# Next block's small parameters and weight diagonals made inside the expert loop, and the second layer's end norm in two VectorE steps

## The chip, the cores and the metric

The kernel runs on one core of one Trainium2 chip. The metric is the device time of one execution in microseconds (us); of several runs the median counts. TensorE does the matrix products, VectorE the elementwise work with two operands, ScalarE activations and casts, GpSimd a third share of elementwise work and the indirect gathers; SyncE's queue issues nearly all other DMA transfers. Each engine works through its own instructions in a fixed order.

## The reference

A stack of three blocks for 512 tokens of width 1024, all in float32. Two layers of a first kind (three mixers side by side, then a mixture of experts), and one of a second kind. What the change touches is the end of each first-kind layer:

```python
for l in range(2):
    ...
    x = _layernorm(DEEPNORM_ALPHA * x + mix, ln1_g[l], ln1_b[l])
    ffn = _hier_moe(x, ...)            # 16 experts, 2 per token, weighted sum
    x = _layernorm(DEEPNORM_ALPHA * x + ffn, ln2_g[l], ln2_b[l])
# second block:
h = rmsnorm(x, norm_mix_w_2)           # x is needed too, for the residual
proj = h @ w_in_2
```

## The kernel before

Tokens lie in four tiles (NT = 4) of 128 partitions, `R[:, i]` being one tile of 128x1024 values. Matrix products are made of three passes on values split in a high and a low part (lines 122 to 124); a weight unit is loaded as float32 into `raw`, cast by ScalarE to the high part (line 132) and subtracted by VectorE or GpSimd for the low part (line 137). A few weight units sit in rings, and a cast waits until TensorE has let go of the ring's oldest unit.

`layer(l)` does one first-kind layer. After the routing (`route`, lines 1146 and following) it emits the loop of 16 experts: for each expert the 96 token rows are gathered by GpSimd from `Xd` (line 1072), transposed by TensorE (line 1079), run through gate, up and down products, and stored to `Yd` by SyncE (line 2038). The loop is software-pipelined: step `s` issues the gather of expert `s`, the transposes of `s-1`, the gate and up products of `s-2` and the down products of `s-3`.

Behind the loop, in program text, stand the small things of the next block. `cols` (lines 150 to 161) loads some rows of 128 values into one buffer `colr` (line 155), transposes them on TensorE into the PSUM pool `tr`, which the experts' transposes use too (line 158), and copies them out on VectorE (line 160); `colr` has one buffer, so each `cols` waits until the one before it has been transposed. `gc2` holds the norm's columns. `params(l + 1)` (line 1926) is eight or so small loads and two more `cols`, `cw` and `gcol`. In the second layer there are also the diagonals `dg`: eight 128x128 tiles, the identity times one token weight, made by GpSimd (line 2066) from the routing weights `w`.

Instructions are not run in the order of the text: a scheduler places each on its engine's queue when its own model of time says that the operands are there, and takes what stands first in the text when several are ready. So an instruction can be placed far ahead of its place in the text, and text order is a priority.

Behind a conditional block for overflowing experts (line 2072) comes the end of the layer. GpSimd gathers each token's two expert rows from `Yd` (line 2085). In the second layer token tiles 0 and 1 are summed on VectorE (lines 2091 and 2092), tiles 2 and 3 on TensorE with the diagonals (line 2099) and added by VectorE (line 2100). Then `moments` (line 440) makes the negative mean `nm`, the sum of squares on ScalarE (line 450) and the inverse deviation `rs` on VectorE in eight small steps (lines 169 to 177). The normed value is made by VectorE's product `nm*rs` (2104), ScalarE's Identity pass (2105), VectorE's product with the gain (2110) and GpSimd's sum with the bias (2111). ScalarE squares that (line 1308), VectorE makes the inverse root mean square, GpSimd the diagonal `rd` from it (2114), and `to_T` (line 336) transposes the tile with `rd` on TensorE (347) and splits it on ScalarE and VectorE (356, 357). The first loads of the next weights are gated (line 225): they wait until the last token tile's buffer `Yg[3][0]`, in which line 1308 also leaves its squares, is free.

Of the kernel before, what the change touches and what calls it, by code (L numbers as in the profile page):

```python
# [11 lines left out]
AF = mybir.ActivationFunctionType  # L12
OP = mybir.AluOpType
AX = mybir.AxisListType

P = 128
S = 512
NT = S // P
D = 1024
KD = D // P  # L20
# [48 lines left out]
class Kernel:  # L69
# [1894 lines left out]
    def layer(self, l):  # L1964
        nc, tc, a, v = self.nc, self.tc, self.a, self.nc.vector
# [3 lines left out]
        with ExitStack() as c:  # L1969
            mo = self.pool(c, f"moe{l}")  # L1970
# [4 lines left out]
            if l:  # L1975

                gb = [self.t(mo, "Ye", [P, D], bufs=2) for _ in range(2)]
# [8 lines left out]
            gb = halves()  # L1986
            gb = [gb[:, z] for z in range(2)]
# [3 lines left out]
            rw, bias, gc = self.router_weights(l, mo)  # L1991
# [42 lines left out]
            wts, rows, PM, cnt = self.route(mo, LG)  # L2034
            n = nc.values_load(cnt[0:1, 0:1], min_val=0, max_val=S)

            ex = {}
            store = lambda e: lambda y: nc.sync.dma_start(self.Yd[e * CAP:e * CAP + CAP, :], y)
            for s in range(16 + 4):
                if s == 8 and l == 0:  # L2040
                    self.level_masks(self.t(mo, "GTh", [P, KD, P], bufs=2))
                if s == 0:
                    self.pat = [("act", "dve")]

                if s < 16:
                    idx = self.slot_ids(mo, PM[:, s, :], 0, "idx")
                    ex[s] = self.expert(mo, [self.part((l, z, s)) for z in "gud"], idx, store(s))
                    next(ex[s])
                for z in (1, 2, 3):
                    if s - z in ex:  # L2050
                        next(ex[s - z])
            if l == 1:
                gb = halves()
                gb = [gb[:, z] for z in range(2)]
                for t, nm in zip(gb, ("ln2_g", "ln2_b")):
                    self.bcast_load(t, a[nm][l], D)
            fp = lambda ap: ap.rearrange("(f p) -> f p", p=P)
            if l == 0:
                gc = self.cols(self.ppool, "gc2", [fp(a["ln2_g"][l]), fp(a["ln2_b"][l])], 2 * KD)
            else:  # L2060
                gc = self.cols(self.ppool, "gc2", [fp(a["norm_mix_w_2"][0])], KD, 2 * KD)

                dg = self.t(mo, "dg", [P, 2, NT, P])
                for j in range(2):
                    for i in range(NT):
                        nc.gpsimd.tensor_tensor(dg[:, j, i], self.ident, wts[j][:, i:i + 1].to_broadcast([P, P]), op=OP.mult)
            self.params(l + 1)
            self.set_phase("m", [self.raw0], [self.ring0], [("act", "dve")])
            x2.close()
            x2 = ExitStack()  # L2070
# [17 lines left out]
            for i in range(NT):  # L2088
                r = R[:, i]
                if l == 0 or i < 2:  # L2090
                    v.scalar_tensor_tensor(r, Yg[i][0], wts[0][:, i:i + 1], r, op0=OP.mult, op1=OP.add)
                    v.scalar_tensor_tensor(r, Yg[i][1], wts[1][:, i:i + 1], r, op0=OP.mult, op1=OP.add,
                                           accum_out=sums[:, i, 0:1])
                else:
                    for hf in range(2):
                        py = self.ps(("pg", "py")[hf], [P, 512])
                        hs = slice(hf * 512, (hf + 1) * 512)
                        for j in range(2):
                            nc.tensor.matmul(py, dg[:, j, i], Yg[i][j][:, hs], start=j == 0, stop=j == 1)
                        v.scalar_tensor_tensor(r[:, hs], py, 1.0, r[:, hs], op0=OP.mult, op1=OP.add,  # L2100
                                               accum_out=sums[:, i, hf:hf + 1])
                nm, rs = self.moments(mo, r, sums[:, i, 0:1 if l == 0 or i < 2 else 2], Yg[i][0], 0.5e-5, nc.gpsimd if i < 2 and l == 0 else v)
                xh = Yg[i][1]
                v.tensor_tensor(nm, nm, rs, op=OP.mult)
                nc.scalar.activation(xh, r, AF.Identity, scale=rs, bias=nm)
                if l == 0:
                    nc.sync.dma_start(self.X2d[tok(i), :], xh)
                    self.to_T(XT, xh, i, gc=gc[:, 0:KD], bc=gc[:, KD:2 * KD], pool=mo)
                    continue
                v.tensor_tensor(r, xh, gb[0], op=OP.mult)  # L2110
                nc.gpsimd.tensor_tensor(r, r, gb[1], op=OP.add)
                rs = self.rms(mo, None, r, None, jk=Yg[i][0])
                rd = self.t(mo, "ehh", [P, 2, P], bufs=2)[:, 0]
                nc.gpsimd.tensor_tensor(rd, self.ident, rs.to_broadcast([P, P]), op=OP.mult)
                nc.sync.dma_start(self.X2d[tok(i), :], r)
                self.dump("x2_1", r, i)
                self.to_T(XT, r, i, gc=gc, pool=mo, rs=rd)
# [34 lines left out]
```

## Time and profile before

| what | before |
|---|---|
| median of 3 runs | 1753.94 us (1753.11 to 1755.02) |
| the profiled execution's own time | 1757.97 us |
| its span, first to last instruction | 1756.2 us |
| TensorE busy | 1598.3 us (91%) |
| VectorE busy | 1157.4 us (66%) |
| ScalarE busy | 808.5 us (46%) |
| GpSimd busy | 646.7 us (37%) |
| mean granted TensorE clock | 0.952 of full speed |

Times in the rows are microseconds from the start of the span. PE is TensorE, PEld its weight load, DVE VectorE, ACT ScalarE, POOL GpSimd, SPq SyncE's queue. L2104 is line 2104 of the kernel. "x4" behind a row counts instructions. What stands in brackets behind a row of a timeline is how long the engine was idle before it, and what ended that.

### The profile page before, as it was taken

The page shows a single profiled execution, that of the slowest core. Times are in us where ns is not written, and L with a number is a line of the kernel's source. Part 1 is how long each engine was busy: PE and PEld are TensorE (multiplying, and loading weights), DVE is VectorE, ACT ScalarE, POOL GpSimd, SP SyncE. Part 2 cuts the span into 40 slices and gives each one's busy share as a digit, 9 for nine tenths or more (in the row PEclk, how much of TensorE's full clock was granted, in tenths as well). Part 3 has the DMA queues.
Part 4 walks back from the last instruction along what each step waited for, and adds up shares of the span by engine and source line. Part 5 has one row for each costly group of instructions (what it writes and reads, how often), then busy time and mean ns, then how long its engine had stood idle before and what let it go on. Part 6 is the DMA issues. An engine that isn't in the chain of part 4 may idle for free. (4 is left out here: it accounts for less than half of the span.)

```text
span 1756.2 us, 28416 instructions
## 1 busy us (share of the span) xinstructions
PE 1598.3 (91%) x11003; PEld 1393.3 (79%) x11003; DVE 1157.4 (66%) x2327; ACT 808.5 (46%) x1396; POOL 646.7 (37%) x515
## 2 busy tenths in 40 slices
PE   7899999799976999998889995999798899999997
PEld 6789889788965789888879973887578788888886
DVE  3866963789967947865689977778774543333334
ACT  3344562267855344551358874465442432222221
POOL 1455331315005445334325204117533534444440
PEclk9999999889997999998989997999899999999999
DMA  5213324499956211124399964432112423333301
GB/s 156 85 58 111 98 76 120 171 340 365 374 185 211 76 57 35 61 84 135 124 336 356 378 238 154 126 96 73 38 51 85 148 92 96 96 96 96 96 25 48
DMA packets 126839, 247.95 MB, mean 141 GB/s; under 512 B 27180, under 2 KB 90470, under 8 KB 114406
## 3 DMA queue, kind: packets, MB, share of 16 engines
q1 hardware_dynamic: 120806, 225.05, 37.4%
q0 software_dynamic: 5888, 20.97, 3.8%
q8 instruction: 90, 1.47, 0.3%
q14 instruction: 55, 0.45, 0.1%
HBM read 218.21 MB, written 27.79 MB: 140 GB/s over the span
## 5 line engine op out<-in xcount | busy, mean ns | idle before, releaser
L137 POOL TENSOR_TENSOR wl<-raw,wh 128x1024 fp32r<-128x1024 f32 (+4 forms) x157 | 360.4, 2309 | 520.1 <-ACT wh L132 510.2
L132 ACT CAST wh<-raw 128x1024 fp32r<-128x1024 f32 (+3 forms) x361 | 362.6, 1023 | 295.5 <-PE dn L124 98.3
L137 DVE TENSOR_TENSOR wl<-raw,wh 128x1024 fp32r<-128x1024 f32 (+3 forms) x204 | 241.7, 1209 | 32.2 <-ACT wh L132 31.5
L122 PE MATMUL mm<-wh,actTh 128*128 128x256 f32 (+2 forms) x640 | 191.6, 300 | 12.2 <-DVE R L2003 5.8
L124 PE MATMUL mm<-wh,actTl 128*128 128x256 f32 (+2 forms) x640 | 188.1, 296 | 4.2 <-POOL actTl L137 3.3
L123 PE MATMUL mm<-wl,actTh 128*128 128x256 f32 (+2 forms) x640 | 188.2, 294 | 0.5 <-DVE wl L137 0.3
L122 PE MATMUL mm<-actTh,wh 128*128 128x512 f32 x368 | 150.0, 408 | 6.1 <-ACT xp L568 3.3
L123 PE MATMUL mm<-actTl,wh 128*128 128x512 f32 x368 | 147.8, 402 | 0.0
L124 PE MATMUL mm<-actTh,wl 128*128 128x512 f32 x368 | 147.6, 401 | 0.0
L122 PEld LDWEIGHTS mm<-wh,actTh 128*128 128x128 f32 x640 | 126.6, 198 | 15.4 <-DVE R L2003 6.0
L124 PEld LDWEIGHTS mm<-wh,actTl 128*128 128x128 f32 x640 | 126.1, 198 | 7.9 <-POOL actTl L137 4.5
L123 PEld LDWEIGHTS mm<-wl,actTh 128*128 128x128 f32 x640 | 127.0, 198 | 2.1 <-issue 0.8
L1751 DVE TENSOR_TENSOR u<-rl 128x512 f32<-128x512 f32 x32 | 52.4, 1636 | 114.4 <-ACT rl L1750 114.4
L1072 POOL DMA_INDIRECT G<-Xd,idx x32 | 74.0, 2312 | 127.0 <-DVE oh L1120 58.8
L1766 DVE TENSOR_TENSOR R<-R,dn 128x512 f32<-128x512 f32 x64 | 43.8, 684 | 94.5 <-PE dn L124 94.4
L122 PE MATMUL mm<-mTh,wh 128*128 128x512 f32 x256 | 100.8, 394 | 0.4 <-ACT mTh L132 0.4
L122 PE MATMUL dn<-wh,uTh 128*128 128x512 f32 x256 | 101.1, 395 | 0.0
L123 PE MATMUL dn<-wl,uTh 128*128 128x512 f32 x256 | 101.1, 395 | 0.0
L124 PE MATMUL dn<-wh,uTl 128*128 128x512 f32 x256 | 101.0, 394 | 0.0
L123 PE MATMUL mm<-mTl,wh 128*128 128x512 f32 x256 | 100.5, 392 | 0.0
L124 PE MATMUL mm<-mTh,wl 128*128 128x512 f32 x256 | 100.4, 392 | 0.0
L122 PEld LDWEIGHTS mm<-actTh,wh 128*128 128x128 f32 x368 | 70.5, 192 | 21.8 <-ACT xp L568 3.9
(699 smaller groups left out, 4016.1 us busy)
## 6 DMA issues: line engine op xcount, KB each, us to landing
raw<-in_expert_w_gate_dram SPq DMA_DIRECT2D x32, 1024.0 KB
raw<-in_expert_w_up_dram SPq DMA_DIRECT2D x32, 1024.0 KB
raw<-in_expert_w_down_dram SPq DMA_DIRECT2D x32, 1024.0 KB
raw<-in_w_ff_dram SPq DMA_DIRECT2D x32, 1024.0 KB
raw<-in_w_in_dram SPq DMA_DIRECT2D x27, 1024.0 KB
raw<-in_w_out_dram SPq DMA_DIRECT2D x12, 1024.0 KB
Yd<-Ye SPq DMA_DIRECT2D x32, 384.0 KB
Yd<-zr SPq DMA_DIRECT2D x9, 512.0 KB
```

The source lines that it names most:

```text
L122: mm(out, lhsT.h, rhs.h, start=start, stop=False, **kw)
L123: mm(out, lhsT.h, rhs.l, start=False, stop=False, **kw)
L124: mm(out, lhsT.l, rhs.h, start=False, stop=stop, **kw)
L132: nc.scalar.copy(dst.h, src)
L137: (nc.gpsimd if leng == "pool" else nc.vector).tensor_tensor(dst.l, src, dst.h, op=OP.subtract)
L1072: nc.gpsimd.indirect_dma_start(out=G[:n], out_offset=None, in_=self.Xd, in_offset=bass.IndirectOffsetOnAxis(ap=idx[:n], axis=0))
L1751: v.tensor_tensor(u, r, r, op=OP.mult)
L1766: v.tensor_tensor(r, r, p, op=OP.add)
```

## The change

The small parameters of the next block (`gc2` and `params(l + 1)`) stand at the head of step 10 of the expert loop in the text, in both layers, where they stood behind the loop. The eight diagonals `dg` stand there too in the second layer, and are made by ScalarE's Copy with a scale column and no longer by GpSimd. In the second layer's end norm two VectorE steps, (r + nm) * gain and (that * rs) + bias, replace VectorE's product `nm*rs`, ScalarE's Identity pass, VectorE's product with the gain and GpSimd's sum. The diagonal `rd` is made by ScalarE and no longer by GpSimd. The first layer's end norm keeps its steps.

```diff
             for s in range(16 + 4):
 ...
+                if s == 10:
+                    if l == 0:
+                        gc = self.cols(self.ppool, "gc2", [fp(a["ln2_g"][l]), fp(a["ln2_b"][l])], 2 * KD)
+                    else:
+                        gc = self.cols(self.ppool, "gc2", [fp(a["norm_mix_w_2"][0])], KD, 2 * KD)
+                        dg = self.t(mo, "dg", [P, 2, NT, P])
+                        for j in range(2):
+                            for i in range(NT):
+                                nc.scalar.activation(dg[:, j, i], self.ident, AF.Copy, scale=wts[j][:, i:i + 1])
+                    self.params(l + 1)
 ...
-            if l == 0:
-                gc = self.cols(self.ppool, "gc2", [fp(a["ln2_g"][l]), fp(a["ln2_b"][l])], 2 * KD)
-            else:
-                gc = self.cols(self.ppool, "gc2", [fp(a["norm_mix_w_2"][0])], KD, 2 * KD)
-                dg = self.t(mo, "dg", [P, 2, NT, P])
-                for j in range(2):
-                    for i in range(NT):
-                        nc.gpsimd.tensor_tensor(dg[:, j, i], self.ident, wts[j][:, i:i + 1].to_broadcast([P, P]), op=OP.mult)
-            self.params(l + 1)
 ...
                 xh = Yg[i][1]
-                v.tensor_tensor(nm, nm, rs, op=OP.mult)
-                nc.scalar.activation(xh, r, AF.Identity, scale=rs, bias=nm)
                 if l == 0:
+                    v.tensor_tensor(nm, nm, rs, op=OP.mult)
+                    nc.scalar.activation(xh, r, AF.Identity, scale=rs, bias=nm)
 ...
-                v.tensor_tensor(r, xh, gb[0], op=OP.mult)
-                nc.gpsimd.tensor_tensor(r, r, gb[1], op=OP.add)
+                v.scalar_tensor_tensor(xh, r, nm, gb[0], op0=OP.add, op1=OP.mult)
+                v.scalar_tensor_tensor(r, xh, rs, gb[1], op0=OP.mult, op1=OP.add)
                 rs = self.rms(mo, None, r, None, jk=Yg[i][0])
                 rd = self.t(mo, "ehh", [P, 2, P], bufs=2)[:, 0]
-                nc.gpsimd.tensor_tensor(rd, self.ident, rs.to_broadcast([P, P]), op=OP.mult)
+                nc.scalar.activation(rd, self.ident, AF.Copy, scale=rs)
```

## Rows read from the trace of the kernel before

**Rows 1.** Page, part 1: span, and busy time of each engine (share) xinstructions.
```profile
span 1756.2 us, 28416 instructions
PE 1598.3 (91%) x11003; PEld 1393.3 (79%) x11003; DVE 1157.4 (66%) x2327; ACT 808.5 (46%) x1396; POOL 646.7 (37%) x515
```
**Rows 2.** Busy time by stretch, second layer's expert loop; the columns are the first line.
```profile
core 0: us, PE busy (x) PEld busy (x) DVE busy (x) ACT busy (x) POOL busy (x), PEclk, DMA share, GB/s
890.00:1020.00 130.00, 129.66 (x999) 119.85 (x999) 121.86 (x168) 104.36 (x155) 36.47 (x16) 0.99 1.01 370
```
**Rows 3.** Waits in 890 to 1020: who for whom, total us, times, longest.
```profile
ACT wh L132 <- PE pg L124: 8.6, 10, 1.7
...
SPq L232 <- DVE wl L137: 52.7, 25, 4.0
```
**Rows 4.** Timeline of PE and POOL, first layer: start, us, instruction; loop's start and end.
```profile
345.76 0.17 PE L1200 MATMUL sm<-Mb,triS 128*128 128x16 bf16 x1 [7.62 <-DVE Mb L1195]
...
348.50 1.33 POOL L1072 DMA_INDIRECT G<-Xd,idx  x1 [5.86 <-DVE idx L1126]
...
352.94 1.54 PE L1079 MATMUL tr<-ident,G 96*128 96x96 f32 x8 [2.66 <-DMA G<-Xd,idx]
...
517.66 0.39 PE L124 MATMUL mm<-wh,hTl 128*96 128x512 f32 x1
```
**Rows 5.** The same for the second layer, with ACT.
```profile
878.88 0.17 PE L1200 MATMUL sm<-Mb,triS 128*128 128x16 bf16 x1 [7.60 <-DVE Mb L1195]
...
879.40 3.85 POOL L2066 TENSOR_TENSOR dg<-ident,w 128x128 f32<-128x128 f32 x8 [3.72 <-DVE w L1187]
883.41 1.01 POOL L1072 DMA_INDIRECT G<-Xd,idx  x1 [0.17 <-DVE idx L1126]
...
887.68 1.54 PE L1079 MATMUL tr<-ident,G 96*128 96x96 f32 x8 [3.08 <-DMA G<-Xd,idx]
...
888.62 0.48 ACT L132 CAST GTh<-tr 128x384 fp32r<-128x384 f32 x1 [9.99 <-PE tr L1079]
...
1052.44 0.39 PE L124 MATMUL mm<-wh,hTl 128*96 128x512 f32 x1
```
**Rows 6.** Chain of waits that ended last, second layer's end: start, us, what.
```profile
1070.52 1.25 ACT GTl L2105
...
1073.49 1.98 DVE lnnm L2104
...
1088.09 1.82 DVE lnnm L2104
...
1092.51 2.38 POOL R L2111
```
**Rows 7.** Groups by line, 1062 to 1112: xcount | busy us, mean ns | idle before.
```profile
L2110 DVE TENSOR_TENSOR R<-G,raw 128x1024 f32<-128x1024 f32 x2 | 2.5, 1226 | 0.7 <-ACT G L2105 0.7
...
L2092 DVE SCALAR_TENSOR_TENSOR R<-G,w,R 128x1024 f32<-128x1024 f32 x1 | 1.3, 1284 | 0.0
...
L2104 DVE TENSOR_TENSOR lnnm<-lnnm,lnrs 128x1 f32<-128x1 f32 x4 | 4.2, 1041 | 0.0
...
L356 ACT ACTIVATE actTh<-tr,gc 128x128 fp32r<-128x128 f32 x30 | 10.3, 365 | 8.5 <-DVE actTl L357 4.8 <-PE tr L347 3.6
```
**Rows 8.** Busy time by stretch (columns as in Rows 2): second layer's end.
```profile
1068.34:1111.80 43.46, 34.77 (x167) 26.12 (x168) 34.07 (x129) 25.01 (x53) 13.46 (x17) 0.81 0.36 129
```
**Rows 9.** All of line 158 in 485 to 520: shortest/median/longest ns.
```profile
L158 PE MATMUL tr<-ident,colr x3: 220/229/248, 492.0 to 513.6; 16*128 16x16 f32 x1, 36*128 36x36 f32 x1, 3*128 3x3 f32 x1
```
**Rows 10.** Last expert load on SP's queue, and the stretch behind it (columns as Rows 2).
```profile
1012.23 0.33 SPq L232 DMA_DIRECT2D raw<-in_expert_w_down_dram  x1
...
1012.56:1028.00 15.44, 15.15 (x117) 13.77 (x115) 13.77 (x21) 11.58 (x19) 0.00 (x0) 1.00 1.00 404
```
**Rows 11.** Timeline of SP and PE near the start: a small load and its transpose.
```profile
38.28 0.35 SPq L155 DMA_DIRECT2D colr<-in_mla_kv_norm_dram  x1
...
42.27 0.22 PE L158 MATMUL tr<-ident,colr 3*128 3x3 f32 x1
```

More of the change, by code (lines that the diff above doesn't have):

```diff
@@ L2037, in layer @@
             ex = {}
+            fp = lambda ap: ap.rearrange("(f p) -> f p", p=P)
             store = lambda e: lambda y: nc.sync.dma_start(self.Yd[e * CAP:e * CAP + CAP, :], y)
@@ L2056, in layer @@
                     self.bcast_load(t, a[nm][l], D)
-            fp = lambda ap: ap.rearrange("(f p) -> f p", p=P)
-            if l == 0:
-                gc = self.cols(self.ppool, "gc2", [fp(a["ln2_g"][l]), fp(a["ln2_b"][l])], 2 * KD)
-            else:
-                gc = self.cols(self.ppool, "gc2", [fp(a["norm_mix_w_2"][0])], KD, 2 * KD)
-                dg = self.t(mo, "dg", [P, 2, NT, P])
-                for j in range(2):
-                    for i in range(NT):
-                        nc.gpsimd.tensor_tensor(dg[:, j, i], self.ident, wts[j][:, i:i + 1].to_broadcast([P, P]), op=OP.mult)
-            self.params(l + 1)
             self.set_phase("m", [self.raw0], [self.ring0], [("act", "dve")])
```

## The prediction

> **What bounds the kernel now.** I read the page first: TensorE is busy for 91% of the span [rows 1], so the question for every edit is whether it shortens a stretch in which TensorE waits. Then the busy time by stretch. In the second layer's expert loop TensorE is busy for 129.66 of 130 us [rows 2]. The waits there say the same: ScalarE's casts wait for TensorE to free a weight unit, and the queue of loads waits for buffers to be emptied, 25 times and up to 4.0 us [rows 3]; no engine waits there for a weight that has not come. So nothing that is moved into this loop makes TensorE faster, and nothing that takes other engines' idle time slows it. TensorE waits at three other places that the change touches: before the first expert of the second layer, between the last expert and the end norm (which no edit shortens), and in the end norm up to the next projection. These I took from the timeline and from the chain of waits.
>
> **Part 1, the diagonals leave GpSimd.** The trace shows both layers starting their expert loops with the same code, except that the second has the eight diagonals. The scheduler had put these not behind the loop but right behind the routing: GpSimd makes them from 879.40 for 3.85 us, and the first gather follows at 883.41 [rows 5]. Count from the routing's first matmul: in the first layer the first gather comes 348.50 - 345.76 = 2.74 us after it and the first transposes 352.94 - 345.76 = 7.18 us [rows 4]; in the second 4.53 us and 887.68 - 878.88 = 8.80 us [rows 5]. The difference in the transposes, 1.62 us, is what the diagonals cost. The loops are equally long from there: 518.05 - 352.94 = 165.11 us and 1052.83 - 887.68 = 165.15 us, so an earlier start is an earlier end. On ScalarE the diagonals cost about 8 x 0.365 = 2.9 us by the 128x128 row of line 356 [rows 7]; ScalarE is idle for 9.99 us before its first cast [rows 5], the weights are there when GpSimd now takes them, and a scheduler that put them forward on one idle engine will do so on another. That hides them; if instead they stay at step 10, ScalarE is busy for 104 of 130 us there [rows 2], and the 2.9 us still lie beside TensorE's work. I take **1.6 us less**. The ends are 0 (the gathered rows land no sooner, since loads fill the DMA engines) and 1.8 (the difference of the gathers).
>
> **Part 2, the small parameters move into the loop.** Loads that wait for nothing but a free buffer were already placed much earlier, so moving their text moves nothing. What moves are the three transposes of each layer, which stand behind the experts' in the pool `tr`, their VectorE copies, and four groups of loads: those of `cw` and `gcol` in each layer, each of which waits on SyncE's queue for the transpose before it. On TensorE three transposes cost 3 x 0.23 = 0.7 us [rows 9], now at the loop's end, then in its middle: TensorE is full in both, so **0**. If the small gaps at the loop's end cover them now, they cost up to 0.7 us a layer, 1.4 in all; if they stand in the way of something there, as much is gained. SyncE's queue can stand still behind such a load; what queues behind it are weight loads, which now wait for buffers themselves [rows 3], so that a few us are covered. What is not covered is TensorE waiting for a load that lands late; that is the slower rival below.
>
> **Part 3, the end norm.** The chain of waits from 1070 to 1096 goes through ScalarE's Identity pass of 1.25 us three times (one row stands), through VectorE's product of single columns twice, at 1.98 and 1.82 us, through the product with the gain four times, and at the end through GpSimd's sum of 2.38 us, behind which line 1308 squares and the gated weight load starts [rows 6]. Removed from this chain: 3 x 1.25 + 1.98 + 1.82 + 2.38 = 9.93, and 4 products of 1.23 = 4.9 [rows 7]. Added: 8 steps of two operands and a column. The nearest row is line 2092, the same operation on the same size, at 1.284 us [rows 7]; the product's 1.23 is the other end, and makes 0.4 us of difference over eight. I take 8 x 1.28 = 10.24. On the chain this is -9.93 - 4.9 + 10.24 = -4.6 us.
>
> But VectorE has other work that the chain does not show, the small steps of `rs` and the splits of line 357. Its own account: out go the four products, 4.9, and line 2104, 4.2 for four instructions [rows 7]; in come 10.24. So it has 1.1 us more to do, in a stretch in which it is busy for 34.07 of 43.46 us [rows 8]. I take the chain less this: -4.6 + 1.1 = **3.5 us less**. The ends: if VectorE were the only limit and all its idle time went, the stretch would shrink to 34.07 + 1.1 = 35.2 us, 8.3 less; if everything removed was hidden, it grows by 1.1. What is late next, where the stall goes: VectorE itself, with the splits of `to_T`. The diagonal `rd` is 0.40 us on GpSimd and by line 356 0.37 on ScalarE: 0, and ScalarE, rid of four passes of 1.25, has the room. The first layer's norm is not changed.
>
> The row that surprises is line 2104: one value per partition, yet twice nearly 2 us, and at 1041 ns on the mean [rows 7]. Beside both long ones GpSimd's sum of line 2111 is running. The Trainium skill (SBUF — State Buffer, section "Who interferes with whom") says that a VectorE instruction with two SBUF inputs and a GpSimd instruction that reads SBUF exclude each other, the later one standing still until the other is done. The trace agrees. By the rule the stall goes with GpSimd's sum, and Part 3 stays as it is; if it were only the place where another wait becomes visible, its 3.5 us would come back behind the new steps and Part 3 would be nil, 1752.3 in all. The rule also says that the new steps are open to the same stall, having two SBUF inputs each; GpSimd then has only two one-element copies left in this stretch.
>
> **The sum.** -1.6 + 0 - 3.5 = -5.1 us. The profiled execution took 1757.97 us itself, 1.8 more than its span; it would take 1752.9. It lies 4.03 us above the median of the runs; put against that median, 1753.94 - 5.1 = **1748.8 us**.
>
> **The rivals.**
>
> *Slower: TensorE waits in the loop for a small load.* The load of `cw` is issued only when `gc2` has been transposed, and lands behind the weight loads queued before it. How many are these? After the last expert load was issued at 1012.23, traffic held 404 GB/s until 1028 [rows 10], 6.2 MB; 1.5 MB were issued behind it (264 columns of the next weights, 1.08 MB, and one store of 0.39 MB), so 4.7 MB stood ahead, 11.7 us. TensorE keeps its order: if the transpose was placed sooner than that behind its load, TensorE stands still. For it: near the start the order left only 42.27 - 38.63 = 3.6 us [rows 11]. Against it: there TensorE ran into no wait, with one load of 1 MB ahead, so the placing seems to know of a queue. Price: 11.7 - 3.6 = 8.1 us for each of four loads, up to 1748.8 + 32 = 1781; one load makes 1756.9, two make 1765. It decides from the second late load on. Chance 0.13. The Trainium skill (DMA: Bandwidth & Descriptors, section "Queues, rings and completion order") says that each DMA engine takes the descriptors of one queue in ring order; no row here shows the landing of a small load in the loop, and without that order the price would be nil.
>
> *VectorE is the bound of the end norm.* For it: 34.07 of 43.46 us, and idle time that is partly the gap between dependent small steps. Against it: the waits of TensorE and ScalarE in the same stretch. Then Part 3 is +1.1: 1753.94 - 1.6 + 1.1 = 1753.4. Chance 0.20.
>
> *The loop starts no sooner.* For it: the loads that fill the DMA engines when the first gather is issued. Against it: the first layer, with the same loads. Then only Part 3: 1750.4. Chance 0.14.
>
> *The gaps close wholly.* -1.6 - 8.3: 1744.0. TensorE waits for ScalarE, VectorE or GpSimd all along this stretch, and its granted clock is 0.81 there [rows 8], between its levels of 1.2 and 2.4 GHz, so that fewer gaps could pay twice. Chance 0.08.
>
> **How the numbers follow.** The forecast has 0.45. A measurement of this kernel can tell about 0.2%, 3.5 us, from no change: faster ends at 1750.4, slower begins at 1757.5. Faster: 0.38 of the forecast's 0.45 (the rest of it is a Part 3 below 2 us), half of the third rival's 0.14, and 0.08 of the fourth: 0.53. Slower: the first rival and 0.01 for the moved transposes: 0.14. The rest, 0.33, is within. The range runs from the fourth rival to just above one late load: 1744 to 1758; what is left out is two or more late loads, about 0.1, and some 0.05 below.
>
> **What would show it.** Part 1: no GpSimd work between routing and first gather, the first transposes of the second layer about 7.2 us behind the routing's first matmul, the eight diagonals on ScalarE before its first cast. Part 2: TensorE still full from 890 to 1020, no wait of line 158 for `colr`. Part 3: no VectorE instruction of one column over 1 us, the stretch of rows 8, from the first matmul with the diagonals to the first full matmuls of the next projection, 3.5 us shorter; if the splits of line 357 follow each other without gaps there, VectorE is the bound and the second rival holds. The prediction is wrong if TensorE shows waits of several us at line 158, or if the order of the loop has changed so much that its 165 us differ.

## The result

The changed kernel took **1777.84 us** (median of four runs, 1771.73 to 1780.71), the kernel before 1754.48 beside it; the ratio is 1.0126, 95% interval 1.0096 to 1.0156. It is 1.3% slower, about 22 us by the ratio, where 5.1 us less were forecast. The profiled execution is the shortest of the four, 1771.73 us with a span of 1770.0, so the two profiles differ by 13.8 us only. They show where the time went all the same. Part 1 of the page after, to be read against rows 1:

```profile
span 1770.0 us, 28380 instructions
PE 1599.2 (90%) x11003; PEld 1392.6 (79%) x11003; DVE 1157.8 (65%) x2327; ACT 808.6 (46%) x1404; POOL 631.0 (36%) x499
```

No engine has more to do. By stages (first or last matmul of each stage in the timelines of TensorE):

| stage | before | after | difference |
|---|---|---|---|
| start to the first layer's routing | 345.76 | 345.31 | -0.45 |
| routing to first transposes, first layer | 7.18 | 8.05 | +0.87 |
| expert loop, first layer | 165.11 | 172.79 | **+7.68** |
| to the second layer's routing | 360.83 | 359.86 | -0.97 |
| routing to first transposes, second layer | 8.80 | 7.26 | -1.54 |
| expert loop, second layer | 165.15 | 175.34 | **+10.19** |
| wait for the gathered rows | 15.51 | 15.75 | +0.24 |
| end norm (the stretch of rows 8) | 43.46 | 42.60 | -0.86 |
| the rest | 644.40 | 643.04 | -1.36 |

The loss lies in the two expert loops, 17.9 us. Busy time by stretch, the loops of the kernel before first (columns as in the first line):

```profile
core 0: us, PE busy (x) PEld busy (x) DVE busy (x) ACT busy (x) POOL busy (x), PEclk, DMA share, GB/s
352.94:518.05 165.11, 160.98 (x1171) 145.42 (x1171) 147.15 (x217) 127.12 (x188) 34.76 (x28) 0.96 0.91 327
887.68:1052.83 165.15, 161.39 (x1171) 145.48 (x1171) 146.27 (x203) 127.22 (x188) 37.38 (x17) 0.96 0.91 333
```

and of the kernel after: the two loops, the end norm, and three short stretches inside the loops:

```profile
353.36:526.15 172.79, 162.89 (x1171) 145.21 (x1171) 148.68 (x217) 128.11 (x188) 31.50 (x28) 0.96 0.87 311
893.27:1068.61 175.34, 163.57 (x1171) 146.22 (x1171) 147.13 (x206) 128.02 (x188) 40.47 (x17) 0.94 0.88 313
1084.36:1126.96 42.60, 33.36 (x164) 25.51 (x164) 33.21 (x126) 20.96 (x54) 2.18 (x9) 0.84 0.37 131
440.00:456.00 16.00, 11.22 (x42) 6.93 (x43) 9.96 (x17) 8.69 (x14) 0.34 (x1) 0.79 1.01 419
980.00:996.00 16.00, 8.92 (x32) 5.39 (x33) 7.90 (x14) 6.88 (x11) 0.00 (x0) 0.78 1.02 376
996.00:1003.00 7.00, 7.00 (x37) 6.58 (x37) 2.93 (x6) 2.96 (x5) 1.67 (x2) 0.52 1.01 395
```

The matmuls are the same 1171. TensorE's idle time grew from 165.11 - 160.98 = 4.1 to 9.9 us and from 3.8 to 11.8 us, and its busy time by 1.9 and 2.2 us. Matmuls run slower behind idle time: from 996 to 1003, after a wait of 5.4 us, the granted clock is 0.52, the lower of the two levels (1.2 GHz). Nearly all of the new idle time is at 438 to 457 (5.4 us idle) and 978 to 1003 (8.7 us), where the small parameters now stand. Timeline of TensorE in the first layer, the transposes of the experts (L1079) and of the small parameters (L158), and the other instructions that waited:

```profile
421.84 0.58 PE L1079 MATMUL tr<-ident,G 96*128 96x96 f32 x4
...
429.85 0.23 PE L158 MATMUL tr<-ident,colr 16*128 16x16 f32 x1
...
439.69 0.25 PE L158 MATMUL tr<-ident,colr 36*128 36x36 f32 x1 [0.57 <-DMA colr<-in_ssd_conv_w_dram]
441.45 0.47 PE L122 MATMUL mm<-wh,hTh 128*96 128x512 f32 x1 [1.51 <-ACT hTh L132]
...
444.23 0.55 PE L1096 MATMUL ht<-ident,ehh 96*128 96x96 f32 x2 [1.61 <-DVE cw L1956]
...
452.16 0.22 PE L158 MATMUL tr<-ident,colr 3*128 3x3 f32 x1
452.32 0.68 PE L1079 MATMUL tr<-ident,G 96*128 96x96 f32 x4
454.70 0.68 PE L1079 MATMUL tr<-ident,G 96*128 96x96 f32 x4 [1.70 <-DVE gcol L160]
```

Only 0.57 us of this is TensorE standing at a small load. The 1.61 and 1.70 us are waits for VectorE's steps on the small parameters, the scaling of `cw` and the copy of `gcol` out of `tr`. And between 421.84 and 452.32, 30.5 us, no expert is transposed; in the kernel before the longest such interval is 12.7 us. The next experts' transposes follow the small ones in the pool `tr`, and the small ones follow each other at the pace of a load each. Without transposes there are no new gate and up products. What TensorE has left between the gate and up products of one expert and the next is down products, and one of these waits for the split of its operand (the 1.51 us). In the second layer the same, and worse at the last group, where TensorE does stand at the load, for 5.40 us:

```profile
961.04 0.58 PE L1079 MATMUL tr<-ident,G 96*128 96x96 f32 x4
...
968.50 0.22 PE L158 MATMUL tr<-ident,colr 8*128 8x8 f32 x1
...
978.11 0.26 PE L158 MATMUL tr<-ident,colr 48*128 48x48 f32 x1
...
995.58 0.28 PE L158 MATMUL tr<-ident,colr 32*128 32x32 f32 x1 [5.40 <-DMA colr<-in_lru_a_param_dram]
995.80 1.54 PE L1079 MATMUL tr<-ident,G 96*128 96x96 f32 x8
```

SyncE's queue in that stretch shows why that group is late:

```profile
968.76 0.33 SPq L155 DMA_DIRECT2D colr<-in_gdn_conv_w_dram  x1
...
980.21 0.38 SPq L155 DMA_DIRECT2D colr<-in_lru_conv_w_dram  x1
...
981.51 0.25 SPq L155 DMA_DIRECT2D colr<-in_lru_gate_a_b_dram  x1
984.96 0.25 SPq L155 DMA_DIRECT2D colr<-in_lru_gate_x_b_dram  x1
988.61 0.25 SPq L155 DMA_DIRECT2D colr<-in_lru_a_param_dram  x1
991.11 0.36 SPq L232 DMA_DIRECT2D raw<-in_expert_w_up_dram  x1
```

Its waits from 981 to 989, for whom, us, times, longest:

```profile
SPq L155 <- DMA raw<-in_expert_w_up_dram: 3.4, 1, 3.4
SPq L155 <- DMA raw<-in_expert_w_down_dram: 3.2, 1, 3.2
```

The group is five loads. The last two are each held back until an earlier weight load has ended, those issued at 970.43 and 973.07. Counted along the queue, each waits for the transfer issued eight places before it. In the packed traces of both kernels the queue's transfers signal eight semaphores in turn, so this is a wait of the program's own: five small loads take five of the eight places. The weight load behind them, at 991.11, had a wait of 2.2 us of its own. It delays nothing that the trace shows: in neither loop does an engine wait for an expert's weight to land, so late weight loads are not the cause. In the kernel before, where this group stands at the loop's end, its loads follow each other without such waits, and the data is there less than 3 us after the last (SyncE's queue, then TensorE):

```profile
1045.30 0.29 SPq L155 DMA_DIRECT2D colr<-in_lru_a_param_dram  x1
```

```profile
1048.11 0.25 PE L158 MATMUL tr<-ident,colr 32*128 32x32 f32 x1
```

In the loop after, the transposes that had to wait for their load came 439.69 - 430.54 = 9.2 and 995.58 - 988.61 = 7.0 us behind the last issue of their group.

### The profile page after: what moved, and what is told of

Its sections match the earlier page's. It is cut to its first block, busy times and chain, and to the rows that moved or that the text cites. A ratio compares the mean times of both kernels' runs of the same rounds, so it can differ in the third digit from the quotient of the medians.

```text
span 1770.0 us, 28380 instructions
## 1 busy us (share of the span) xinstructions
PE 1599.2 (90%) x11003; PEld 1392.6 (79%) x11003; DVE 1157.8 (65%) x2327; ACT 808.6 (46%) x1404; POOL 631.0 (36%) x499
```

## The experiments

Two theories stood at the start. **Late loads**: the small parameters carry the whole loss, since each group's load is issued only behind the transpose of the group before. **Together**: the loss comes from the diagonals and the end norm, or needs all three parts. First each part alone, then the two others without the small parameters.

**The small parameters alone.** Kernel before, with `gc2` and `params(l + 1)` at step 10:

```diff
+                if s == 10:
+                    if l == 0:
+                        gc = self.cols(self.ppool, "gc2", [fp(a["ln2_g"][l]), fp(a["ln2_b"][l])], 2 * KD)
+                    else:
+                        gc = self.cols(self.ppool, "gc2", [fp(a["norm_mix_w_2"][0])], KD, 2 * KD)
+                    self.params(l + 1)
```

> The small parameters at step 10 of the loop alone; diagonals and end norm as before. Theory (late small loads hold TensorE, the rest of the change is not at fault): +18 to +27 us by the time, the whole loss and a little more, with waits of several us at line 158 or behind it in both layers and loops some 7 and 10 us longer. Rival (the loss comes from the eight diagonals on ScalarE at step 10 together with the end norm, or needs all three): under +5 us.

Measured: 1776.03 us beside 1755.56; ratio 1.0115 (1.0096 to 1.0133), that is +20.2 us. The loops take 173.12 and 173.89 us, the longest intervals between experts' transposes are 30.2 and 33.7 us. TensorE's longest waits in its two stretches, second layer (960 to 1005), then first (415 to 460):

```profile
PE tr L158 <- DMA colr<-in_lru_conv_w_dram: 4.8, 1, 4.8
PE tr L158 <- DMA colr<-in_gdn_conv_w_dram: 2.1, 1, 2.1
...
PE mm L122 <- ACT hTh L132: 2.2, 1, 2.2
PE tr L1079 <- DVE gcol L160: 1.7, 1, 1.7
PE ht L1096 <- DVE cw L1956: 1.3, 1, 1.3
```

This part carries the loss; "together" falls. In the second layer TensorE's two waits at line 158 make 6.9 us, about as much as its idle time in that loop grew by (3.8 to 10.8 us). In the first layer TensorE waits at none of the three.

**Without the small parameters.** The whole change, but the small parameters stay behind the loop:

```diff
-                        nc.gpsimd.tensor_tensor(dg[:, j, i], self.ident, wts[j][:, i:i + 1].to_broadcast([P, P]), op=OP.mult)
+                        nc.scalar.activation(dg[:, j, i], self.ident, AF.Copy, scale=wts[j][:, i:i + 1])
 ...  (and the end norm as in the change)
```

> The diagonals on ScalarE and the end norm in two steps, small parameters behind the loop as before. Theory: -1.6 and -0.9, about -2.5 us, so 1751 to 1752. By the prediction's steps for these two parts: -5.1, so 1749. Rival (these two parts carry the loss): slower than before by over 5 us.

Measured: 1750.54 us beside 1755.56; ratio 0.9967 (0.9955 to 0.9978), -5.8 us with an interval of -7.9 to -3.9. The loops take 162.83 and 161.29 us. The two parts don't add up to the whole: 20.2 - 5.8 = 14.4 us, beside 22 us for the change. Why the 5.8 us don't show beside the late loads is open.

**The end norm alone** and **the diagonals alone**, each the lines of the change by themselves:

```diff
-                nc.scalar.activation(xh, r, AF.Identity, scale=rs, bias=nm)
 ...
+                v.scalar_tensor_tensor(xh, r, nm, gb[0], op0=OP.add, op1=OP.mult)
+                v.scalar_tensor_tensor(r, xh, rs, gb[1], op0=OP.mult, op1=OP.add)
 ...
+                nc.scalar.activation(rd, self.ident, AF.Copy, scale=rs)
```

> The end norm in two VectorE steps alone, the rest as before. Theory (VectorE is nearly without a gap in this stretch, so that the shorter chain pays little): about -0.9 us, as the stretch from the first diagonal matmul to the first full projection matmul shrank from 43.46 to 42.60 us in the changed kernel. Rival (the prediction's step): -3.5 us, hidden in the changed kernel by the later loads. The first would be seen as 1753 to 1754 us, the second as 1750 to 1751.

> The eight diagonals on ScalarE alone, at their old place in the text. Theory: -1.6 us, the first transposes of the second layer 7.2 us behind the routing's first matmul (8.80 before), and the loop of 165.15 us as long as before. Rival: the earlier start is given back in the loop, whose 165.15 us grow by 1.5, and the time is the same.

Measured: end norm 1753.61 beside 1755.56, ratio 0.9984 (0.9969 to 0.9998); diagonals 1752.45, ratio 0.9984 (0.9972 to 0.9997). The first lies between what the two theories gave, and neither differs by more than the unchanged kernel does from itself (last run below). So the times don't settle single parts of this size; the stages have to. For the diagonals they do: from routing to first transposes 7.36 us with ScalarE, and the loop (163.82 us) gives nothing back.

**One group behind.** As the first experiment, but the second layer's last group, `gcol` with its five loads, stays behind the loop:

```diff
             r["cw"] = self.cols(m, "cw", ...)
-            r["lc"] = self.cols(m, "gcol", [a["lru_conv_w_2"][0]..., ...], 32, 32)
 ...
+            if l == 1:
+                self.lru_cols()
             self.set_phase("m", [self.raw0], [self.ring0], [("act", "dve")])
```

> Small parameters at step 10 alone, but the second layer's last group (five loads, one transpose) stays behind the loop. Theory: the wait for that group in the second layer (5.4 us in the changed kernel) goes with the low clock behind it, so 6 to 9 of the 20 us: +11 to +14. The first layer's loop stays about 8 us longer. Rival (what counts is the order of the loop from the first moved transpose on): no more than 3 us come back.

Measured: 1770.67 us beside 1756.35, ratio 1.0084 (1.0069 to 1.0099), +14.8 us: 5.4 of the 20 us came back, a little less than expected. The longest interval between experts' transposes in the second layer fell from 33.7 to 18.3 us, with two groups in the way and one load to wait for; that loop takes 163.81 us. The first layer's, with its three groups, still has 30.0 us without an expert's transpose, and takes 175.95.

**The loads early.** Same place, same three transposes in the same pool, but the three groups lie in one buffer `colr` at different rows, so no load waits for a transpose:

```diff
+    def cols_all(self, specs, one):
+        r = self.t(self.ppool, "colr", [P, P])
+        at = 0
+        for tag, rows, n, room in specs:
+            for src in rows:
+                self.nc.sync.dma_start(r[at:at + src.shape[0], :], src)
+                at += src.shape[0]
+        o, p = 0, None
+        for tag, rows, n, room in specs:
+            if p is None or not one:
+                p = self.ps("tr", [P, at])
+                self.nc.tensor.transpose(p, r[:at], self.ident[:at, :at])
+            c = self.t(self.ppool, tag, [P, room or n])[:, :n]
+            self.nc.vector.tensor_copy(c, p[:, o:o + n])
+            o += n
+            self.pre[tag] = c
```

> Small parameters at step 10 alone (as in the run of this part by itself), but the three groups of rows lie in one buffer, so that no load waits for a transpose and all are issued long before the loop; three transposes at step 10 as there (each of all the rows). Theory (what costs is that a load is issued only behind a transpose and lands 7 to 9 us later, with the experts' transposes queued behind): the loss of 20 us is gone, within 3 us of before, and TensorE waits at none of the three transposes. Rival (the transposes themselves cost, by taking the experts' turns in the pool tr and changing the order of the loop): 15 us or more stay.

Measured: **1747.52 us** beside 1756.35, ratio 0.9949 (0.9937 to 0.9962). The loss is gone, and 8.8 us more. The loads go out at 41.9 to 45.1 us for the first layer and at 435.0 to 444.6 for the second. TensorE, first layer:

```profile
422.34 0.58 PE L1079 MATMUL tr<-ident,G 96*128 96x96 f32 x4
...
430.37 0.26 PE L2136 MATMUL tr<-ident,colr 55*128 55x55 f32 x1
431.80 0.26 PE L2136 MATMUL tr<-ident,colr 55*128 55x55 f32 x1
434.75 0.27 PE L2136 MATMUL tr<-ident,colr 55*128 55x55 f32 x1
436.47 0.58 PE L1079 MATMUL tr<-ident,G 96*128 96x96 f32 x4
```

The three transposes (L2136 here) pass within 4.4 us, where they took from 429.85 to 452.16. So it isn't the transposes that cost, it is the chain of loads between them. (The edit unchains the loads and moves them far ahead at once; which of the two would do alone was not run.) The loops, columns as above:

```profile
353.72:515.77 162.05, 157.93 (x1171) 142.66 (x1171) 147.50 (x217) 127.20 (x188) 32.52 (x28) 0.99 0.91 332
885.00:1044.50 159.50, 157.17 (x1171) 142.16 (x1171) 145.52 (x203) 126.35 (x188) 33.45 (x17) 0.98 0.93 343
```

**Is that gain of the loads or of the place?** The same early loads in the kernel before with the transposes behind the loop; the whole change with early loads and one transpose; with three; and the change without the moved place but with early loads. The edit, at step 10 or behind the loop, with `one` false or true:

```diff
-                        gc = self.cols(self.ppool, "gc2", [fp(a["norm_mix_w_2"][0])], KD, 2 * KD)
+                        self.cols_all([("gc2", [fp(a["norm_mix_w_2"][0])], KD, 2 * KD)] + self.par_cols(l + 1), False)
+                        gc = self.pre.pop("gc2")
```

> Kernel before with one edit: the three groups of rows lie in one buffer and are loaded long before the loop; their transposes stay behind the loop in the text. The same loads at step 10 made the kernel 0.51% faster than before (loops of 162.1 and 159.5 us for 165.1 and 165.2). Theory A (the gain is of the early loads, since in the kernel before too the last two groups are loaded behind transposes, at the loops' ends): -0.4 to -0.6% here as well. Theory B (the gain is of the place at step 10, where the transposes leave the loop's end): within 0.2% of before.

Measured: 1754.31 beside 1755.89, ratio 0.9990 (0.9981 to 1.0000). Early loads alone are worth nothing that can be told from noise.

> The whole change, with the three groups of rows in one buffer, loaded long before the loop, and transposed at once at step 10 (one transpose, three copies). Theory: as fast as the change without its moved parameters, -0.33% or -5.8 us, so about 1749.7; the place of the parameters is then worth nothing. Rival (the place at step 10 costs by itself): slower than before by 10 us or more.

Measured: **1748.63** beside 1756.35, ratio 0.9952 (0.9939 to 0.9965).

> The whole change with the early loads in one buffer and three transposes at step 10. If the parts add up: -0.51% for the parameters and -0.33% for diagonals and end norm, about -0.8%, 1741 to 1743. If they overlap (the same waits and clock phases are paid only once), -0.5%, as with the single transpose: 1747 to 1748.

Measured: 1751.76 beside 1755.89, ratio 0.9972 (0.9960 to 0.9984).

> Diagonals on ScalarE and end norm in two steps, early loads in one buffer, transposes behind the loop. Theory A (early loads gain by themselves): -0.7 to -0.9%. Theory B (only the place gains): -0.33% as without the early loads, about 1750.

Measured: 1753.48 beside 1755.89, ratio 0.9987 (0.9977 to 0.9998), less of a gain than either theory gave.

By the two kernels without the other parts of the change the place gains and the early loads don't. But the parts don't add up: with diagonals and end norm on top, the same early loads give -0.28 or -0.48%, not -0.8. The loops of these kernels take 161.1 to 166.0 us, with TensorE busy for 157.9 to 161.2 us with the same matmuls, and what they differ by is the granted clock. Of the 22 loops in the eleven profiles without late loads (two of them of the kernel before), the eight with a mean clock of 0.98 or 0.99 keep TensorE busy for 157.1 to 158.4 us, the fourteen with 0.96 or 0.97 for 159.3 to 161.4 us. Of the 8.7 us by which both loops of the kernel with early loads at step 10 are shorter than before, 7.3 us are TensorE's busy time, at 0.99 and 0.98 where the kernel before had 0.96 twice. So that gain, too, is in its profile mostly clock. Whether the order of a kernel brings a higher clock or the execution does is not shown; the last run bears on it.

**The long one-column product.** Kernel before, with the sum on VectorE:

```diff
-                nc.gpsimd.tensor_tensor(r, r, gb[1], op=OP.add)
+                v.tensor_tensor(r, r, gb[1], op=OP.add)
```

> Kernel before with one edit: the sum with the bias in the second layer's end norm goes from GpSimd to VectorE. Theory (the one-column product is held up by GpSimd's sum running beside it): the product's 1.98 and 1.82 us fall to the 0.16 of its short instances, and the time is within 3 us of before, since VectorE takes four sums of 1.2 us. Rival (the long duration is another wait that only becomes visible there): one of the four stays above 1 us.

Measured: 1757.45 beside 1756.35, ratio 0.9996 (0.9982 to 1.0009). All four products of the second layer are short now (group by line, xcount | busy us, mean ns):

```profile
L2104 DVE TENSOR_TENSOR lnnm<-lnnm,lnrs 128x1 f32<-128x1 f32 x4 | 0.6, 153 | 0.0
```

Of the 4.2 us of rows 7, 3.6 were the stall beside GpSimd's sum. The Trainium skill (SBUF — State Buffer, section "Who interferes with whom") says that a VectorE instruction with two SBUF inputs and a GpSimd instruction that reads SBUF exclude each other; this agrees. The stretch of rows 8 became longer all the same, 46.40 us. VectorE has four sums of 1.22 us more and 3.6 us of stall less, but its busy time there grew by 0.8 us only (34.07 to 34.87); what the rest is was not found.

**The kernel before once more.** No edit.

> The kernel before, unchanged, profiled and timed once more, as a measure of what two executions of one program differ by. The kernels without late loads have expert loops of 159.5 to 166.0 us, and TensorE is busy there for 157.1 to 161.4 us with the same matmuls, at granted clocks of 0.96 to 0.99. Theory (which short gaps at a loop's end are followed by low clock differs from execution to execution): the ratio is 1 within 0.15%, but a loop or another stage differs from the first profile by 1.5 us or more. Rival (stage lengths belong to the order of a kernel): all stages within 0.5 us of the first profile.

Measured: 1754.44 beside 1756.35, ratio 0.9985 (0.9972 to 0.9999), for the same program. Its loops:

```profile
353.98:519.34 165.36, 161.28 (x1171) 145.66 (x1171) 147.15 (x217) 127.22 (x188) 30.78 (x28) 0.96 0.91 327
889.22:1052.21 162.99, 159.57 (x1171) 144.08 (x1171) 145.98 (x203) 127.31 (x188) 37.39 (x17) 0.97 0.92 336
```

The second loop is 2.2 us shorter than in the first profile, the end norm 1.8 us (41.64). The loop's end shows where most of the 1.8 us of TensorE's busy time went. In both profiles TensorE waits there 1.09 us for the same step of VectorE (`wl`, line 137), up to 1039.25 in the first profile and 1040.14 in this one. The 5 us behind that wait, first profile, then this one:

```profile
1039.25:1044.25 5.00, 5.00 (x26) 4.56 (x27) 2.89 (x5) 2.29 (x4) 0.00 (x0) 0.66 0.93 294
1040.14:1045.14 5.00, 5.00 (x33) 4.23 (x34) 3.67 (x6) 3.30 (x6) 0.00 (x0) 1.00 0.98 310
```

The same program ran on at a granted clock of 0.66, partly at the lower level, in one execution and at 1.00 in the other. So a ratio within 0.3% of 1 may mean nothing here, whatever its interval says, and a stage of one profile is known to 2 us at best, unless it repeats. By this measure the 0.33% of the change without the small parameters is at the edge, the 0.5% of two of the kernels with early loads beyond it.

## Why the prediction was wrong

- **What bounds the kernel.** That "nothing that takes other engines' idle time slows it" was the error in the reading. TensorE was full in 890 to 1020 [rows 2] because a next expert's transposes always came in time. Their order in the pool `tr` is a resource of its own, and no view of busy time shows it.
- **Part 1** was right: diagonals on ScalarE at 886.48, right behind the routing, the first gather 2.72 us behind the routing's first matmul, the first transposes 7.26 us behind it (forecast 2.74 and 7.18). Timeline after, to be read against rows 5:

```profile
886.01 0.17 PE L1200 MATMUL sm<-Mb,triS 128*128 128x16 bf16 x1 [7.60 <-DVE Mb L1195]
...
886.48 2.45 ACT L2055 ACTIVATE dg<-ident,w 128x128 f32<-128x128 f32 x8 [0.72 <-DVE w L1187]
888.73 1.25 POOL L1072 DMA_INDIRECT G<-Xd,idx  x1 [5.92 <-DVE idx L1126]
...
893.27 1.06 PE L1079 MATMUL tr<-ident,G 96*128 96x96 f32 x5 [2.81 <-DMA G<-Xd,idx]
```

  It repeats: all six kernels with ScalarE's diagonals have 7.2 to 7.5 us here, all eight with GpSimd's 8.8 to 9.1. The -1.6 us hold as -1.5.
- **Part 2 is the step that failed.** It was costed at 0, with TensorE's transposes at 0.23 us each; it is worth +20 us. The text had seen both halves: that the loads of `cw` and `gcol` wait for the transpose before, and that the transposes stand in the experts' pool. It didn't put them together: three transposes, each behind a load, hold up every expert behind them for the sum of the loads, 30.5 and 34.8 us without an expert's transpose where 12.7 was the most before. That "a few us are covered" was true of SyncE's queue, not of this.
- **The first rival** happened, at a chance of 0.13. Its backlog was near: it took 11.7 us from a load's issue to its landing, and the transposes that waited, in three kernels with late loads, came 6.3 to 11.3 us behind the last issue of their group. Its upper end, 1781, held. It looked for the price at TensorE standing by a small load, and that is most of the second layer's new idle time (5.40 us after, 6.9 us with the small parameters alone). In the first layer it is 0.57 us or none, and there it is luck that the upper end holds: the loss is in the missing transposes, with dependent down products, in the waits for VectorE's steps, and in the low clock behind the gaps. The reason given against it, that the placing knows of a queue, was right for the distance between a load and its transpose, and no help: in the first layer the second and third transposes were placed 9 and 12 us behind their loads, and that is what kept the experts waiting.
- **Ring order.** The Trainium skill (DMA: Bandwidth & Descriptors, section "Queues, rings and completion order") says that the descriptors of one ring are taken in order. The traces are in line with it, but don't show the order by itself: less than 3 us from issue to transpose where the DMA engines have little to do (share 0.23 in 1043.89 to 1048.11 before), 7 to 9 us in the loop after, where they are full (share 1.01 and 1.02 in the stretches above).
- **Part 3** was too large. The stretch of rows 8 shrank by 0.86 us, not 3.5. Over six profiles with the new norm it takes 40.8 to 44.4 us, over seven with the old one 41.6 to 45.7 (the sum on VectorE left out); the means, 42.6 and 43.3, differ by less than the scatter. The second rival, VectorE as the bound, comes nearer in size, but isn't shown: VectorE's busy time went from 34.07 to 33.21, where the prediction's account gave 1.1 more, and it is idle for 9.4 us as before. What the sum left out is order. The eight small steps that make a tile's inverse root mean square stand on VectorE's queue, and the new passes of 1.28 us over other tiles stand between them (at 1091.79 and 1094.87): for the first tile they take 1097.06 - 1091.05 = 6.0 us from first start to last end, where they took 3.3 before. That repeats, with 6.0 to 6.3 us in all six profiles with the new norm and 2.6 to 3.3 us in the seven with the old. And `rd` on ScalarE was costed at 0, but here it stands in ScalarE's queue behind a squares pass of another tile. VectorE, then ScalarE, then TensorE after:

```profile
1091.05 0.14 DVE L169 TENSOR_SCALAR rmrq_h<-rmss 128x1 f32<-128x1 f32 x1
...
1096.86 0.20 DVE L177 TENSOR_SCALAR rmrs<-rmrq_w,rmrq_y 128x1 f32<-128x1 f32 x1
```

```profile
1097.58 1.13 ACT L450 ACTIVATE GTh<-R,lnnm 128x1024 f32<-128x1024 f32 x1
...
1098.71 0.39 ACT L2116 ACTIVATE ehh<-ident,rmrs 128x128 f32<-128x128 f32 x1
```

```profile
1099.15 3.78 PE L347 MATMUL tr<-ehh,R 128*128 128x128 f32 x16 [5.18 <-ACT ehh L2116]
```

  The inverse root is ready at 1097.06, the diagonal begins 1.65 us later, and TensorE had waited 5.18 us for it, 1.71 us before. The 1.65 us don't repeat as the 6 us do: over the six profiles they are 0.03 to 1.65 us. And TensorE's wait varies with the old norm too, from 1.7 to 4.5 us, against 3.1 to 5.2 us with the new.
- **The sum of Parts 1 and 3**, -5.1, stands beside a measured -5.8 (-7.9 to -3.9). By the stages only the 1.5 us of Part 1 in it are shown, so the agreement is luck as far as the traces go: the loops are shorter by 6 us in that profile, with TensorE busy for 6.9 us less at clocks of 0.98 and 0.99, and the clock is what varies from execution to execution.
- **The bound of 0.2%** for what can be told was barely wide enough: the same program differed from itself by 0.15%, with an interval that reaches 0.28%.

## What to carry to other kernels

A small load with its transpose is cheap only while nothing stands behind it in order: before moving such a thing into a full loop, ask which pool and which queue it joins, and whether its load is issued early or only when the one before is through. Chained loads through one buffer cost the loop the time from a load's issue to its transpose each, waited for or planned by the scheduler (6 to 12 us here), for which the pool's other users stand still; one buffer for all groups, loaded ahead, made the same move free. And run the unchanged kernel against itself before believing a tenth of a per cent, and read the granted clock of a stage before crediting a change with its time.

## What the runs showed of the hardware

- A small load issued into the loop's traffic (DMA share 0.92 to 1.02) was usable 6.3 to 11.3 us behind its issue, and in less than 3 us at a share of 0.23. What held some of them back before the issue (3.4 and 3.2 us in the second layer after) was the program's own wait for a transfer eight places earlier; where those had ended, five went out within 1.7 us (1043.89 to 1045.30, plus the last issue's 0.29).
- The same 1171 matmuls of an expert loop keep TensorE busy for 157.1 to 161.4 us in kernels without late loads, at mean granted clocks of 0.99 down to 0.96; the unchanged kernel shows 161.39 and 159.57 for one loop in two executions. The same wait of 1.09 us was followed by the lower level in one of them and not in the other.
- The one-value VectorE product beside GpSimd's sum takes 1.97 and 1.89 us, and 0.15 us without it.
